# Token differences ahead of their rounding, seven-product blocks on PSUM copies, and attention squares added on GpSimd

## Chip, core and metric

One core of one Trainium2 chip runs the whole program: TensorE (PE in the profile, with its weight loads as PEld), VectorE (DVE), ScalarE (ACT), GpSimd (POOL), and SyncE (SP), whose queue issues the transfers from HBM. The metric is the device time of one execution in microseconds (us). Every number is fp32; a fp32 product is made here as three products of a faster type (below).

## The reference, cut to what matters

One layer: 128 context tokens and 512 latent tokens of 1024 features. The changed places are the sum of squares of the attention's output (the first `_rms` of the mixer) and the SwiGLU network.

```
def _rms(x, g):
    return x * rsqrt(mean(x * x, axis=-1) + 1e-6) * g

# mixer: attn (tokens x 512) and y_conv (tokens x 512) are normed apart, joined and projected
merged = concat([_rms(attn, attn_out_norm), _rms(y_conv, conv_out_norm)])
x = x + g1 * (merged @ w_out)

# feed-forward: w_gate_up 1024 x 5632, w_down 2816 x 1024
h2 = _rms(x, norm_ffn) * (1 + sc2) + sh2
gate, up = split(h2 @ w_gate_up, 2)
x = x + g2 * ((silu(gate) * up) @ w_down)
```

## The kernel before

**Products.** Each fp32 operand is held as a high part, rounded by ACT (L151: `hi = Copy(src)` into type fp32r), and a low part, made by DVE (L152: `lo = src - hi`). `mm3` (L154 to L157) issues hi·hi, hi·lo and lo·hi into one PSUM tile. So every operand costs one ACT and one DVE instruction before TensorE may use it.

**Stages.** The preamble makes the conditioning and the input projections. Then comes the attention stage, with the convolution's products as filler between the attention's steps. After it come the output projection with its residual and the second norm (L1083 to L1147), and the feed-forward part (from L1159) until the end. Tokens go in five blocks of 128: four latent ones, t = 0 to 3, and the context, t = 4.

**What sets the order.** TensorE's order is the order of the program text; in the attention stage it is a list of steps written out by hand (`SEQ`: scores `S`, transposes `T`, value products `O`, filler `F`, sums of squares `r`). On the other engines a scheduler orders instructions by priority; `with early(n)` raises that priority. DVE's order is by hand only from the first feed-forward block until the second call of `b_sums`. Weights go through one list, `order`: `W(key)` gives an entry's tiles and, on the way, loads entries up to `AOP` places further on. An entry is a transfer (rings `w`, `f`) or, for the ring `op`, an operand that `op_load` makes out of weights that lie in SBUF already. Raw weights have three buffers (`wf`); high and low parts have four each (`wh`, `wl`).

**Sums of squares.** For each token block and each half v of the heads, `att_add` (L885) adds two halves of the attention's output on DVE (L895), one after a swap of partitions by DMA, and squares the result on ACT into two of the four 128 x 128 quarters of `osq` (L896; for token block 3 the tile is named `oz`). At step `r`, `att_rms` (L942) sums the squares over the features: four products of 128 x 1 with a vector of ones (L945, two PE rows each, since they stay fp32). DVE scales the sum, and POOL raises it to the power -1/2 (L165). There are five such sites: steps r4, r0, r1, r2 in `SEQ`, and token block 3 in the output projection. POOL otherwise adds the convolution's squares (L758).

**Feed-forward blocks.** The 2816 hidden columns go in 22 blocks f of 128, in four groups (0 to 5, 6 to 11, 12 to 16, 17 to 21). After a group, `down` (L1240) multiplies its hidden values `gT` by `w_down`. A block's weights are two transfers of 512 KB, the gate columns g and the up columns u. Each is cut along the contracted features into A11, A12 (of g) and A21, A22 (of u), four chunks of 128 x 128 each. Tokens are cut into two halves of 320, LO and HI, which gives quarters B11, B21 (LO) and B12, B22 (HI) of the normed input. Blocks 0 and 1 are **plain** (`plain`, L1167): four products A11·B11 + A12·B21 and A21·B11 + A22·B21 for LO, later the same four for HI. From block 2 on, seven products do for eight, in Strassen's manner in Winograd's form: A11·B11, S1·T1, S2·T2, A12·B21, S3·T3, A22·T4, S4·B22. S1 to S4 are sums of A's (`op_load`: L206 on DVE, then the rounding by L151 and L152 on 512-wide tiles). T1 to T4 are differences of B's (`b_sums`, L1071: DVE's difference L1078, ACT's rounding L1064, DVE's low part L1065), made once, in two parts of the token range, tokens 128 to 319 and 0 to 127 of each half. `prod` (L1162) issues one product as four `mm3` with 320 columns, 12 PE rows.

A seven-product block runs on TensorE as `ff_a` (A11·B11 into PSUM tile b1), `ff_c` (S1·T1 into b3), `ff_d` (S2·T2 added to b1), `ff_b` (A12·B21 into b2) and `ff_e` (S3·T3 added to b1, A22·T4 into b4, S4·B22 added to b3). Between them ACT copies what b1 holds at three moments into SBUF (`copy_of`, L1193 to L1196: p1, u2, u3; the profile calls these tiles p and u). DVE adds these to the other products: L1209 `cg = b2 + p1`, L1225 `cu = b3 + u3`, L1228 `cu = b4 + u3`, and L1235 `cg = b3 + u2` in `ff_end`, which is called in the next block behind `ff_c`. ACT applies Silu to cg, DVE multiplies it with cu, and `ff_out` (L1184) rounds the result into gT. PSUM has six tiles for all this (`FB`).

## Time and profile before

| | |
|---|---|
| median of 3 runs | 755.47 us (754.89 to 755.61) |
| the profiled execution | 755.84 us |
| its span | 754.0 us |
| mean granted clock of TensorE | 0.999 |
| PE busy | 735.5 us, 98% |
| PEld busy | 661.6 us, 88% |
| DVE busy | 553.2 us, 73% |
| ACT busy | 378.7 us, 50% |
| POOL busy | 42.7 us, 6% |
| 16 DMA engines, hardware queue q1 | 36.5% |

The profile is one execution on the chip. Each instruction is a row: start in us from the span's beginning, duration, engine, line (L), operation, output `<-` inputs by the program's names, shape, and in brackets the engine's idle time before it with what ended it. `x4` says that a row of the time line stands for four instructions. Matmuls are pipelined and their ends are modelled, so starts are surer than ends. The span leaves out 1.8 us of the execution around it (755.84 - 754.0).

### The profile page before, as it was taken

Reading aid. Unit: us, or ns where it says so; the run is one execution under the profiler, and the core shown is the slowest. Engines: PE = TensorE matmul, PEld = TensorE weight load, DVE = VectorE, ACT = ScalarE, POOL = GpSimd, SP = SyncE. Lnnn points to the kernel's source line nnn. Section 1 sums busy time; section 2 is a strip of 40 time slices with the busy share of each in tenths; the row PEclk is TensorE's granted clock in tenths of the full one; section 3 lists DMA queues with packets and bytes.
Section 4 is the critical chain, followed back from the end, with each engine's and each line's share of the span. In section 5 each row is a group of like instructions: output and inputs, shape, how many; then the busy total and the mean of one; then the engine's idle time right before and its main releaser. Section 6 shows DMA issues by size and latency. Waiting matters only on the chain.

```text
span 754.0 us, 11900 instructions
## 1 busy us (share of the span) xinstructions
PE 735.5 (98%) x4586; PEld 661.6 (88%) x4586; DVE 553.2 (73%) x1009; ACT 378.7 (50%) x745; POOL 42.7 (6%) x75
## 2 busy tenths in 40 slices
PE   7999899999999999999999999999999999999997
PEld 6668788988988887899998799998889998899986
DVE  5668877666666798779979778884678866788653
ACT  5356777667666534765552135553125541255410
POOL 2403101011000110100000000000000000000000
PEclk9999999999999999999999999999999999999999
DMA  9985133532432464031335223223113132122312
GB/s 290 297 242 155 47 107 97 170 92 91 143 123 91 133 240 123 1 112 56 87 110 178 87 63 106 76 94 112 56 56 109 60 112 82 58 87 83 112 56 84
DMA packets 101389, 84.52 MB, mean 112 GB/s; under 512 B 3502, under 2 KB 81650, under 8 KB 101332
## 3 DMA queue, kind: packets, MB, share of 16 engines
q1 hardware_dynamic: 100980, 83.39, 36.5%
q8 instruction: 36, 0.59, 0.3%
q0 software_dynamic: 352, 0.37, 0.2%
q14 instruction: 21, 0.17, 0.1%
HBM read 79.68 MB, written 2.75 MB: 109 GB/s over the span
## 4 chain that ended last, share of the span: by engine, by line
PE 82%; DVE 8%; ACT 5%; DMA 3%; issue 1%; SPq 0%; POOL 0%; ACTq 0%; DVEq 0%
PE pf L155 17%; PE pf L156 17%; PE pf L157 17%; PE pc L717 3%; PE pc L719 3%; PE pc L718 3%; PE ph L155 2%; PE ph L156 2%; PE ph L157 2%; PE po L873 2%; PE ps L829 2%; PE pt L856 2%; PE pc L388 2%; DMA es<-t 1%; ACT pr L839 1%
## 5 line engine op out<-in xcount | busy, mean ns | idle before, releaser
L151 ACT ACTIVATE wh<-wf 128x512 fp32r<-128x512 f32 (+1 forms) x68 | 55.5, 816 | 81.5 <-PE pf L157 59.9
L155 PE MATMUL pf<-wh,gT 128*128 128x512 f32 (+1 forms) x225 | 86.9, 386 | 0.0
L156 PE MATMUL pf<-wl,gT 128*128 128x512 f32 (+1 forms) x225 | 86.5, 385 | 0.0
L157 PE MATMUL pf<-wh,gT 128*128 128x512 f32 (+1 forms) x225 | 86.5, 384 | 0.0
L717 PE MATMUL pc<-hH,wh 128*128 128x320 f32 x192 | 61.1, 318 | 0.0
L719 PE MATMUL pc<-hH,wl 128*128 128x320 f32 x192 | 59.3, 309 | 0.0
L718 PE MATMUL pc<-hL,wh 128*128 128x320 f32 x192 | 59.3, 309 | 0.0
L152 DVE TENSOR_TENSOR wl<-wf,wh 128x1024 fp32r<-128x1024 f32 (+1 forms) x34 | 39.4, 1160 | 24.9 <-ACT wh L151 21.8
L155 PE MATMUL pf<-T,wh 128*128 128x320 f32 x160 | 49.6, 310 | 0.6 <-ACT u L1196 0.5
L155 PEld LDWEIGHTS pf<-wh,gT 128*128 128x128 f32 x225 | 42.3, 188 | 8.6 <-ACT wh L151 0.2
L157 PEld LDWEIGHTS pf<-wh,gT 128*128 128x128 f32 x225 | 42.3, 188 | 8.5
L156 PEld LDWEIGHTS pf<-wl,gT 128*128 128x128 f32 x225 | 42.3, 188 | 8.4 <-issue 0.2
L155 PE MATMUL pf<-T,wl 128*128 128x320 f32 x160 | 49.4, 309 | 0.0
L156 PE MATMUL pf<-T,wl 128*128 128x320 f32 x160 | 49.4, 309 | 0.0
L157 PE MATMUL pf<-T,wl 128*128 128x320 f32 x160 | 49.4, 309 | 0.0
L156 PE MATMUL pf<-T,wh 128*128 128x320 f32 x160 | 49.4, 309 | 0.0
L157 PE MATMUL pf<-T,wh 128*128 128x320 f32 x160 | 49.4, 309 | 0.0
L155 PE MATMUL pf<-B,wl 128*128 128x320 f32 x152 | 47.1, 310 | 0.0
L157 PE MATMUL pf<-B,wl 128*128 128x320 f32 x152 | 47.0, 309 | 0.0
L156 PE MATMUL pf<-B,wl 128*128 128x320 f32 x152 | 47.0, 309 | 0.0
L155 PE MATMUL pf<-B,wh 128*128 128x320 f32 x136 | 42.2, 310 | 1.5 <-DVE cu L1225 1.5
L1275 DVE TENSOR_TENSOR dm<-pf,g 128x512 f32<-128x512 f32 (+1 forms) x41 | 27.7, 676 | 21.1 <-PE pf L157 21.1
(306 smaller groups left out, 2049.6 us busy)
## 6 DMA issues: line engine op xcount, KB each, us to landing
wf<-in_w_gate_up_dram SPq DMA_DIRECT2D x44, 512.0 KB, 3.9
aw<-in_w_ada_dram SPq DMA_DIRECT2D x24, 512.0 KB, 4.0
wf<-in_w_down_dram SPq DMA_DIRECT2D x20, 512.0 KB, 3.3
wf<-in_w_in_dram SPq DMA_DIRECT2D x18, 512.0 KB, 5.9
af<-in_w_ada_dram SPq DMA_DIRECT2D x32, 256.0 KB, 6.5
x<-in_x_sample_dram SPq DMA_DIRECT2D x8, 512.0 KB, 5.8
wf<-in_w_out_dram SPq DMA_DIRECT2D x8, 512.0 KB, 4.4
wf<-in_w_ada_dram SPq DMA_DIRECT2D x8, 512.0 KB, 3.8
```

The lines of the kernel that those rows point to most:

```text
L151: act.activation(hi, src, AF.Copy)
L152: dve.tensor_tensor(lo, src, f32(hi), ALU.subtract)
L155: pe.matmul(out, lh, rh, start=start, stop=False, skip_group_check=more)
L156: pe.matmul(out, lh, rl, start=False, stop=False, skip_group_check=more)
L157: pe.matmul(out, ll, rh, start=False, stop=stop, skip_group_check=more)
L388: pe.matmul(out[CG * g:CG * (g + 1)], cp[:, k], w, start=(k < 4), stop=(k >= KD - 4), skip_group_check=True)
L717: pe.matmul(acc, wh[:, k], hH[k][:, c0:c0 + n], start=(k == 0), stop=False)
L718: pe.matmul(acc, wh[:, k], hL[k][:, c0:c0 + n], start=False, stop=False)
L719: pe.matmul(acc, wl[:, k], hH[k][:, c0:c0 + n], start=False, stop=(k == KD - 1))
L829: pe.matmul(s2[:, g, :320], q, kk[:, v, P + g * 320:P + (g + 1) * 320], start=(i == 0), stop=(i == 1))
L856: pe.transpose(tp[:, i, h], u[3][h][:, kt * P:(kt + 1) * P], ident)
L1275: dve.tensor_tensor(dm, ps[:, :n], g2[cc][:, oc], ALU.mult)
```

## The change

Three things change.

1. **`b_sums`**: the difference of the next T is made before the rounding of the one before: T1, T2, round T1, T3, round T2, T4, round T3, round T4. The arithmetic stays.
2. **Operands and seven-product blocks.** Operands are made two at a time, in 1024-wide tiles: `A1` (all of g), `A2` (all of u), `S12`, `S34`; only A22 of a seven-product block stays 512 wide. `PAIRS` finds the half. A block of seven products now has four entries of `op` instead of seven, a plain one two instead of four, and `AOP` falls from 9 to 6. In the block, ACT copies b1 behind A11·B11 **into PSUM**, to b2, and A12·B21 adds to it there; Silu reads b2 itself. ACT likewise copies b1 behind S3·T3 into b4, and A22·T4 adds to it; DVE's product reads b4 itself. S1·T1 is copied into SBUF (p5) before S4·B22 adds to b3, and the HI half of cu is b1 + p5. The adds L1209 and L1228 are gone. S4·B22 now runs ahead of A22·T4.
3. **`att_add`, `att_rms`**: after the second half's squares, POOL adds the four quarters to one (256 wide, then 128 wide), and `att_rms` issues one product instead of four.

```diff
 FEND = 2
-AOP = 9
+AOP = 6
 NPLAIN = 2
...
         if name[0] == "S":
-            if name == "S1":
-                sums[f] = T("sx", (P, 2, 4, P), F32, 2)
-            s13, s24 = sums[f][:, 0], sums[f][:, 1]
-            src, x, y, op = {"S1": (s13, a21, a22, ALU.add), "S2": (s24, s13, a11, ALU.subtract),
-                             "S3": (s13, a11, a21, ALU.subtract), "S4": (s24, a12, s24, ALU.subtract)}[name]
+            if name == "S12":
+                sums[f] = T("sx", (P, 8, P), F32, 2)
+            s13, s24 = sums[f][:, 0:4], sums[f][:, 4:8]
             with early(SOP[f >= NPLAIN]):
-                (pool if f < SPO else dve).tensor_tensor(src, x, y, op)
+                for out, x, y, op in {"S12": ((s13, a21, a22, ALU.add), (s24, s13, a11, ALU.subtract)),
+                                      "S34": ((s13, a11, a21, ALU.subtract), (s24, a12, s24, ALU.subtract))}[name]:
+                    dve.tensor_tensor(out, x, y, op)
+            src = sums[f]
         else:
-            src = {"A11": a11, "A12": a12, "A21": a21, "A22": a22}[name]
-        w = T(("wh", "wl")[ops[0] % 2], (P, 2, 4, P), F32R, WHB)
-        ops[0] += 1
+            src = {"A1": g, "A2": u, "A22": a22}[name]
+        if name == "A22":
+            w = T(("wh", "wl")[ops[0] % 2], (P, 2, 4, P), F32R, WHB)
+            ops[0] += 1
+            e[5] = w[:, 0], w[:, 1]
+        else:
+            e[5] = T("wh", (P, 8, P), F32R, WHB), T("wl", (P, 8, P), F32R, WHB)
         with early(SOP[f >= NPLAIN]):
-            split(w[:, 0], w[:, 1], src)
-        e[5] = w
+            split(*e[5], src)
...
     GROUPS = [list(range(a, b)) for a, b in zip(GCUT, GCUT[1:])]
-    PLAIN, PRODS = ("A11", "A12", "A21", "A22"), ("A11", "S1", "S2", "A12", "S3", "A22", "S4")
+    PLAIN, PRODS = ("A1", "A2"), ("A1", "S12", "S34", "A22")
+    PAIRS = {"A11": ("A1", 0), "A12": ("A1", 4), "A21": ("A2", 0), "A22": ("A2", 4),
+             "S1": ("S12", 0), "S2": ("S12", 4), "S3": ("S34", 0), "S4": ("S34", 4)}
...
         act.activation(osq[t][:, 2 * v:2 * v + 2], o, AF.Square)
+        if v:
+            q = osq[t]
+            pool.tensor_tensor(q[:, 0:2], q[:, 0:2], q[:, 2:4], ALU.add)
+            pool.tensor_tensor(q[:, 0], q[:, 0], q[:, 1], ALU.add)
         if t == CTX:
...
         sps = PB((P, 1))
-        for p in range(4):
-            pe.matmul(sps, osq[t][:, p], ones[:, 0:1], start=(p == 0), stop=(p == 3))
+        pe.matmul(sps, osq[t][:, 0], ones[:, 0:1], start=True, stop=True)
         rA[t] = rstd_of(sps, 1, 1.0 / 512, tag="rA")
...
         b11, b12, b21, b22 = (quarter(x, part) for x in ("B11", "B12", "B21", "B22"))
-        last = None
-        for x in ("T1", "T2", "T3", "T4"):
-            w = T("tr", (P, 4, 192), F32, 3)[:, :, :n]
-            y, z = {"T1": (b12, b11), "T2": (b22, last), "T3": (b22, b12), "T4": (b21, last)}[x]
-            dve.tensor_tensor(w, y, z, ALU.subtract)
-            b_put(x, w, part)
-            if x != "T3":
-                last = w
+        w = {}
+
+        def diff(x, y, z):
+            w[x] = T("tr", (P, 4, 192), F32, 3)[:, :, :n]
+            dve.tensor_tensor(w[x], y, z, ALU.subtract)
+
+        diff("T1", b12, b11)
+        diff("T2", b22, w["T1"])
+        b_put("T1", w["T1"], part)
+        diff("T3", b22, b12)
+        b_put("T2", w["T2"], part)
+        diff("T4", b21, w["T2"])
+        b_put("T3", w["T3"], part)
+        b_put("T4", w["T4"], part)
...
     open_pool("Y2", "left", "B22 T1 T2 T3 T4")
-    open_pool("G", "right", "cg cu p1 u2 u3 dm tr")
+    open_pool("G", "right", "cg cu p5 u2 dm tr")
     gT, st, pair = {}, {}, [None]
...
     def prod(out, f, a, b, start=True, stop=True, more=False):
-        w = W(("op", f, a))
+        x, k0 = PAIRS[a] if f < NPLAIN or a != "A22" else (a, 0)
+        wh, wl = W(("op", f, x))
         for k in range(4):
-            mm3(out[:, :HALF], w[:, 0, k], w[:, 1, k], *B[b][k], start and k == 0, stop and k == 3, more)
+            mm3(out[:, :HALF], wh[:, k0 + k], wl[:, k0 + k], *B[b][k], start and k == 0, stop and k == 3, more)
...
     def ff_a(f):
-        b1 = FB()
+        b1, b2 = FB(), FB()
         prod(b1, f, "A11", "B11")
-        cg = T("cg", (P, TOK), F32, 2)
-        st[f] = [b1, copy_of("p1", b1), cg, None, None, None, None]
+        with early(CPP):
+            act.activation(b2[:, :HALF], b1[:, :HALF], AF.Copy)
+        st[f] = [b1, b2, T("cg", (P, TOK), F32, 2), None, None, None]
     def ff_b(f):
-        b2 = FB()
-        prod(b2, f, "A12", "B21")
-        b1, p1, cg = st[f][0:3]
-        dve.tensor_tensor(cg[:, LO], b2[:, :HALF], p1, ALU.add)
-        act.activation(cg[:, LO], cg[:, LO], AF.Silu)
+        b2, cg = st[f][1:3]
+        prod(b2, f, "A12", "B21", start=False, more=True)
+        act.activation(cg[:, LO], b2[:, :HALF], AF.Silu)
     def ff_c(f):
-        st[f][3] = FB()
-        prod(st[f][3], f, "S1", "T1")
+        b3 = st[f][3] = FB()
+        prod(b3, f, "S1", "T1")
+        st[f][4] = copy_of("p5", b3)
...
         prod(st[f][0], f, "S2", "T2", start=False, more=True)
-        st[f][4] = copy_of("u2", st[f][0])
+        st[f][5] = copy_of("u2", st[f][0])
     def ff_e(f):
-        b1, _, cg, b3, u2 = st[f][0:5]
+        b1, _, cg, b3, p5, u2 = st[f]
         prod(b1, f, "S3", "T3", start=False, more=True)
-        u3 = copy_of("u3", b1)
+        b4 = FB()
+        with early(CPP):
+            act.activation(b4[:, :HALF], b1[:, :HALF], AF.Copy)
         cu = T("cu", (P, TOK), F32, 2)
-        dve.tensor_tensor(cu[:, HI], b3[:, :HALF], u3, ALU.add)
-        b4 = FB()
-        prod(b4, f, "A22", "T4")
-        dve.tensor_tensor(cu[:, LO], b4[:, :HALF], u3, ALU.add)
-        dve.tensor_tensor(cu[:, LO], cu[:, LO], cg[:, LO], ALU.mult)
+        dve.tensor_tensor(cu[:, HI], b1[:, :HALF], p5, ALU.add)
         prod(b3, f, "S4", "B22", start=False, more=True)
+        prod(b4, f, "A22", "T4", start=False, more=True)
+        dve.tensor_tensor(cu[:, LO], b4[:, :HALF], cg[:, LO], ALU.mult)
         st[f] = cg, cu, b3, u2
...
     def ff_end(f):
```

The first place where the order of instructions moves is DVE's first preparation of T, around block 0's products (`tr` is a difference, `T1` to `T4` the low parts of the rounded differences, gT_712 and gT_713 hold quarters of the normed input). Before:

```order
L1078 TENSOR_TENSOR tr_849_3984<-gT_712_3273 128x768
L1065 TENSOR_TENSOR T1_850_3986<-tr_849_3984,T1_850_3986 128x4x192
L1078 TENSOR_TENSOR tr_851_3989<-gT_713_3274,tr_849_3984 128x768
L1065 TENSOR_TENSOR T2_852_3991<-tr_851_3989,T2_852_3991 128x4x192
L1078 TENSOR_TENSOR tr_853_3994<-gT_713_3274,gT_712_3273 128x768
L1065 TENSOR_TENSOR T3_854_3996<-tr_853_3994,T3_854_3996 128x4x192
L1078 TENSOR_TENSOR tr_855_3999<-gT_713_3274,tr_851_3989 128x768
L1065 TENSOR_TENSOR T4_856_4001<-tr_855_3999,T4_856_4001 128x4x192
```

The same place now (line numbers in rows of the changed kernel are those of its own file; L1087 is the difference, L1074 the low part):

```order
L1087 TENSOR_TENSOR tr_849_3971<-gT_712_3271 128x768
L1087 TENSOR_TENSOR tr_850_3973<-gT_713_3272,tr_849_3971 128x768
L1074 TENSOR_TENSOR T1_851_3975<-tr_849_3971,T1_851_3975 128x4x192
L1087 TENSOR_TENSOR tr_852_3978<-gT_713_3272,gT_712_3271 128x768
L1074 TENSOR_TENSOR T2_853_3980<-tr_850_3973,T2_853_3980 128x4x192
L1087 TENSOR_TENSOR tr_854_3983<-gT_713_3272,tr_850_3973 128x768
L1074 TENSOR_TENSOR T3_855_3985<-tr_852_3978,T3_855_3985 128x4x192
L1074 TENSOR_TENSOR T4_856_3988<-tr_854_3983,T4_856_3988 128x4x192
```

Each low part now has the next difference between itself and its own difference.

The second place is ACT in block 3. Before, from the copy behind A11·B11 (p1_904) to the copy behind S2·T2 (u2_910); cg_884 is block 2's Silu, gT_908 the rounding of its hidden values, and the wl and wh rows round operands of blocks 3 and 4:

```order
L1196 ACTIVATE p1_904_4366<-pf_899_4345 128x320
L1236 ACTIVATE cg_884_4234<-cg_884_4234 128x320
L151 ACTIVATE wl_907_4371<-sx_906_4369 128x512
L151 ACTIVATE gT_908_4389<-cu_895_4309 128x640
L151 ACTIVATE wh_909_4393<-sx_906_4369 128x512
L1196 ACTIVATE u2_910_4408<-pf_899_4345 128x320
L151 ACTIVATE wl_912_4411<-wf_900_4346 128x512
```

And now, from the copy of b1 into b2 (pf_899) to the copy of b1 into b4 (pf_914); wl_897 is A22 of block 3, wh_907 the rounding of S1 and S2 of block 4, cg_904 block 3's Silu:

```order
L1219 ACTIVATE pf_899_4319<-pf_898_4318 128x320
L151 ACTIVATE wl_897_4302<-wf_883_4199 128x512
L1252 ACTIVATE cg_886_4218<-cg_886_4218 128x320
L1212 ACTIVATE p5_909_4362<-pf_905_4342 128x320
L151 ACTIVATE gT_910_4367<-cu_896_4288 128x640
L151 ACTIVATE wh_907_4346<-sx_906_4343 128x1024
L1212 ACTIVATE u2_911_4382<-pf_898_4318 128x320
L1225 ACTIVATE cg_904_4341<-pf_899_4319 128x320
L1241 ACTIVATE pf_914_4415<-pf_898_4318 128x320
```

Ahead of u2 there now stands one rounding of 1024 columns, of both S1 and S2 of the next block, where there were roundings of 512.

The third place is POOL from the sum of token block 0 to that of token block 2 (rA is the power -1/2 of an attention sum, rB that of the convolution's). Before:

```order
L165 TENSOR_TENSOR rA_633_2867<-ms_632_2865,neghalf_40_176 128x1
L758 TENSOR_TENSOR ysum_174_735<-ysum_174_735,c25_709_3234 128x512
L758 TENSOR_TENSOR ysum_174_735<-ysum_174_735,c25_709_3234 128x128
L165 TENSOR_TENSOR rB_726_3329<-ms_725_3327,neghalf_40_176 128x5
L165 TENSOR_TENSOR rA_748_3411<-ms_747_3409,neghalf_40_176 128x1
```

And now:

```order
L905 TENSOR_TENSOR osq_563_2524<-osq_563_2524 128x256
L906 TENSOR_TENSOR osq_563_2524<-osq_563_2524 128x128
L165 TENSOR_TENSOR rA_633_2863<-ms_632_2861,neghalf_40_176 128x1
L764 TENSOR_TENSOR ysum_174_735<-ysum_174_735,c25_709_3230 128x512
L764 TENSOR_TENSOR ysum_174_735<-ysum_174_735,c25_709_3230 128x128
L905 TENSOR_TENSOR oz_665_3019<-oz_665_3019 128x256
L906 TENSOR_TENSOR oz_665_3019<-oz_665_3019 128x128
L165 TENSOR_TENSOR rB_726_3327<-ms_725_3325,neghalf_40_176 128x5
L165 TENSOR_TENSOR rA_748_3406<-ms_747_3404,neghalf_40_176 128x1
```

Two adds stand ahead of each attention power, and those of token block 3 (oz) behind the convolution's adds.

## The prediction

> **What bounds the kernel now.** The page comes first: where the span goes, and which engine the chain that ended last runs through.
>
> ```profile
> span 754.0 us, 11900 instructions
> PE 735.5 (98%) x4586; PEld 661.6 (88%) x4586; DVE 553.2 (73%) x1009; ACT 378.7 (50%) x745; POOL 42.7 (6%) x75
> PE 82%; DVE 8%; ACT 5%; DMA 3%; issue 1%; SPq 0%; POOL 0%; ACTq 0%; DVEq 0%
> ```
>
> TensorE is the bound. A change can win here only by taking rows out of its queue, or by taking a wait out of it. The table by stretches shows which of the changed stages have waits (columns: PE, PEld, DVE, ACT, POOL busy, clock, DMA share, GB/s).
>
> ```profile
> 120.00:200.00 80.00, 79.83 (x572) 71.61 (x570) 51.95 (x105) 55.05 (x120) 7.02 (x14) 1.00 0.35 111
> 345.00:365.00 20.00, 17.97 (x119) 17.18 (x118) 19.78 (x36) 12.13 (x24) 0.00 (x0) 1.00 0.20 58
> 365.00:420.00 55.00, 55.00 (x331) 51.70 (x330) 46.71 (x75) 22.65 (x39) 0.00 (x0) 1.00 0.49 147
> ```
>
> The attention (120 to 200) and the later seven-product blocks (from 365) keep TensorE full. Only the first seven-product block, block 2, lies in a stretch where TensorE stands still for 2 us, and there DVE is full: 19.78 of 20. TensorE's own waits name the places:
>
> ```profile
> PE pf L155 <- DVE cu L1225: 1.5, 1, 1.5
> PE pf L155 <- ACT u L1196: 0.5, 1, 0.5
> PE pt L945 <- ACT osq L896: 0.4, 1, 0.4
> ```
>
> A matmul's end in the record is modelled, so the true price of the first two is read from the starts of block 2's products (first row of each, in the order A11, S1, S2, A12, S3, A22, S4, then the next block):
>
> ```profile
> 348.77 0.31 PE L155 MATMUL pf<-B,wh 128*128 128x320 f32 x1
> 350.53 0.31 PE L155 MATMUL pf<-T,wl 128*128 128x320 f32 x1
> 352.49 0.42 PE L155 MATMUL pf<-T,wh 128*128 128x320 f32 x1
> 354.36 0.31 PE L155 MATMUL pf<-B,wl 128*128 128x320 f32 x1
> 356.80 0.42 PE L155 MATMUL pf<-T,wh 128*128 128x320 f32 x1 [0.52 <-ACT u L1196]
> 358.65 0.31 PE L155 MATMUL pf<-T,wl 128*128 128x320 f32 x1
> 362.05 0.42 PE L155 MATMUL pf<-B,wh 128*128 128x320 f32 x1 [1.47 <-DVE cu L1225]
> 363.91 0.31 PE L155 MATMUL pf<-B,wl 128*128 128x320 f32 x1
> ```
>
> An undisturbed product takes 350.53 - 348.77 = 1.76 us. The others exceed it by 0.20 (S2 late), 0.11, 0.68 (S3 late), 0.09, 1.64 (S4 late) and 0.10 (the slower rows after each wait): **2.82 us** in all. That is everything the seven-product part can give back.
>
> **Part 1: one sum-of-squares product instead of four.** The last of the five sites (token block 3), and the site of token block 2, where TensorE waited:
>
> ```profile
> 269.36 0.95 PE L945 MATMUL pt<-ones,oz 128*128 128x1 f32 x8
> 270.17 0.48 PE L155 MATMUL ph<-wh,mx 128*128 128x512 f32 x1
> 224.90 0.50 PE L945 MATMUL pt<-ones,osq 128*128 128x1 f32 x4
> 225.77 0.61 PE L945 MATMUL pt<-ones,osq 128*128 128x1 f32 x4 [0.37 <-ACT osq L896]
> 226.24 0.36 PE L873 MATMUL po<-ph,VS 128*128 128x256 f32 x1
> 225.30 0.41 ACT L896 ACTIVATE osq<-of 128x256 f32<-128x256 f32 x1
> 265.34 0.42 ACT L896 ACTIVATE oz<-of 128x256 f32<-128x256 f32 x1 [3.61 <-DVE of L895]
> ```
>
> Each site issues 8 rows (two for each fp32 product) in 270.17 - 269.36 = 0.81 us, 0.10 us a row. Six rows go at each: 0.61 us. At four sites the squares are ready long before TensorE asks, so I count 4 x 0.61 = **-2.43 us**. What follows those sites there (scores, row maximum, exponential) starts from TensorE's own rows, so it moves along with it.
>
> The new GpSimd adds are not in the trace; its adds on the convolution's squares are the nearest rows (512 and 128 wide, by form, and the pair on the time line).
>
> ```profile
> L758 POOL TENSOR_TENSOR ysum<-ysum,c 128x512 f32<-128x512 f32 x3 | 4.7, 1583 | 67.4 <-ACT c L756 67.4
> L758 POOL TENSOR_TENSOR ysum<-ysum,c 128x128 f32<-128x128 f32 x3 | 1.6, 528 | 0.0
> 216.04 1.73 POOL L758 TENSOR_TENSOR ysum<-ysum,c 128x512 f32<-128x512 f32 x2 [19.30 <-ACT c L756]
> 174.06 2.24 POOL L758 TENSOR_TENSOR ysum<-ysum,c 128x512 f32<-128x512 f32 x2 [17.00 <-ACT c L756]
> 173.50 1.23 DVE L152 TENSOR_TENSOR wl<-wf,wh 128x1024 fp32r<-128x1024 f32 x1 [0.39 <-ACT wh L151]
> ```
>
> A straight line through 528 and 1583 ns gives 0.88 us at 256 wide; with the 128-wide add, 1.41 us. The bounds are 384/640 of the pair's 1.73 us, 1.04, and its slow case, 2.24. I take 1.41, which lies between like rows. At the site of token block 2 nothing covers it: the squares end at 225.71, the adds at about 227.20 (0.08 us to start), and with 0.06 us to wake TensorE and two rows of 0.10 the next product starts at 227.46 instead of 226.24: **+1.22 us** (0.85 to 2.05 by the bounds). Behind TensorE's new wait stand the last value product of a unit and the next scores; DVE's scale of the sum waits there too, as it does now. At the other sites the cover is larger; the least is at token block 3, whose squares end at 265.76 and whose product starts at 269.36, 3.6 us, more than the adds at their slowest.
>
> The row at 174.06 took 0.51 us longer than the one at 216.04, and beside it DVE ran a subtraction with two SBUF operands. The Trainium skill (SBUF — State Buffer, section "SBUF: two separate sides") says that such a DVE instruction and a GpSimd instruction that reads SBUF lock each other out for a whole instruction; by it this site could cost as much more as the longest such subtraction, 1.23 us, and the sum would be -2.0 instead of -3.2. That rule fits the two rows, but DVE has only a reciprocal and a scale in that moment, so I keep the sum.
>
> **Part 2: differences ahead of their rounding.** DVE around block 2's preparation, and the late instructions:
>
> ```profile
> 331.78 0.95 DVE L1078 TENSOR_TENSOR tr<-gT 128x768 f32<-128x768 f32 x1
> 333.64 0.96 DVE L1065 TENSOR_TENSOR T<-tr,T 128x768 fp32r<-128x768 f32 x1 [0.91 <-ACT T L1064]
> 334.52 0.95 DVE L1078 TENSOR_TENSOR tr<-gT,tr 128x768 f32<-128x768 f32 x1
> 342.73 0.68 DVE L152 TENSOR_TENSOR wh<-wf,wh 128x512 fp32r<-128x512 f32 x1
> 353.95 0.69 DVE L206 TENSOR_TENSOR sx<-wf,sx 128x512 f32<-128x512 f32 x1
> 361.51 0.49 DVE L1225 TENSOR_TENSOR cu<-pf,u 128x320 f32<-128x320 f32 x1
> 338.21 0.31 PE L155 MATMUL pf<-gT,wh 128*128 128x320 f32 x1
> ```
>
> Now each T costs 334.52 - 331.78 = 2.74 us, of which 0.91 is waiting for ACT's rounding; four take until 342.73. In the new order another difference fills each wait: eight instructions at 0.88 us (333.64 to 334.52), 7.0 us, done at 338.8, 3.9 us earlier. The next work, block 2's A1, can't be much earlier than that: its buffer is one that block 0's second-half products read until 338.21. DVE's queue from 342.73 to S4, the last sum of block 2 (353.95), is 11.2 us of work with next to no wait; about 1 us of it can go ahead, so S4 starts near 350 to 351 instead.
>
> **Part 3: the seven-product blocks.** The forms:
>
> ```profile
> L152 DVE TENSOR_TENSOR wl<-wf,wh 128x1024 fp32r<-128x1024 f32 x20 | 24.5, 1223 | 22.0 <-ACT wh L151 20.7 <-PE pf L157 1.3
> L151 ACT ACTIVATE wh<-wf 128x1024 fp32r<-128x1024 f32 x20 | 21.2, 1060 | 49.6 <-PE pf L157 35.9 <-DMA wf<-in_w_down_dram 9.1 <-issue 2.6
> L1196 ACT ACTIVATE u<-pf 128x320 f32<-128x320 f32 x40 | 17.4, 436 | 30.8 <-PE pf L157 30.8
> wf<-in_w_gate_up_dram SPq DMA_DIRECT2D x8, 512.0 KB, 3.9
> ```
>
> TensorE's products are as many and as long as before. DVE loses two adds of 0.49 us in each block and three instruction starts; ACT gets a fourth copy and three rounding starts fewer. Both have room (46.71 and 22.65 of 55), so this is worth nothing by itself. The waits of block 2 change thus. S4 no longer waits for a DVE add (361.51) but for ACT's copy p5, four products old: 1.74 us go. S3 waits for u2, which now stands behind ACT's rounding of A1(3), released by the same product: 0.95 + 0.44 = 1.4 us, less than the 1.76 us of A12 that covers it. S2's copy stands behind T4's rounding, and that now comes earlier with DVE. So 2.82 us go.
>
> A copy that ACT writes into PSUM has no row; the bounds are L1196's 0.44 us and twice that, and I take 0.44, a copy of equal size out of the same memory. S4 (1.76 us) covers the copy that A22 waits for, so at twice the price it shows only where ACT starts it late, 0.4 us a place. No reading below nothing: a faster copy frees nothing that waits.
>
> **What is late next** is block 3's u2. In the new order it stands behind the rounding of S1 and S2 of block 4, which needs those sums, which need up(4) landed; that transfer waits for a buffer that S4's sum of block 3 gives back. With every product at 1.76 us, S3(3) is due at 368.13. The step before: u(3) is asked for after S4(2), 351.6, lands at 355.5 (3.9 us); then A1(3), the sums and S12(3) on DVE and ACT put S4(3)'s end at 361.7; up(4) lands at 365.65; S1, a product and S2 on DVE take until 367.3; the rounding lets go at 368.35, and u2 ends at 368.8. S3(3) waits 0.7 us, 0.8 with the slower rows behind it: **+0.8 us**. From block 4 on DVE has caught up: a block takes TensorE 7 x 1.76 = 12.3 us, and in the stretch from 365 on DVE is busy 46.71 of 55, before it loses two adds of 0.49 a block. I count nothing there.
>
> **Sum.** -2.43 + 1.22 - 2.82 + 0.8 = **-3.2 us** on the profiled execution's 755.84 us (span 754.0 and 1.8 around it): 752.6. That execution lies 0.37 above the median of the runs shown, 755.47; with it the median becomes 752.3, and I say **752.4**.
>
> **Rivals.**
> - All gains, no new wait: up(4) lands earlier or the adds are at their short bound: -2.43 + 0.85 - 2.82 = -4.4, with a shorter wake-up -4.8: 750.7. For it: DVE has 8 us to spare in each later stretch.
> - The attention swallows its part: after a freed slot TensorE only waits longer for an exponential. Then part 1 is +1.22 alone, the whole -0.8: 754.7, no change. For it: two of the chain's engines there are DVE and ACT; against it: 79.83 of 80.
> - **Slower**: u2 stands behind a 1024-wide rounding in each of the 16 blocks that have a successor in their group, and the wait of block 3 comes back in all: 15 more times 0.8 is +12, sum +8.8: 764.3. It decides from 0.31 us a block on (4.7 us over 15). Against it: DVE's slack from 365 on.
>
> **How the numbers follow.** Chances: forecast 0.52, all gains 0.13, swallowed 0.17, slower 0.18. A measurement of this kernel tells about 0.2%, 1.5 us, from no change. Faster is the first two, 0.65; same 0.17; slower 0.18. The range, 750.0 to 755.6, holds the first three cases with the bounds of the adds (-0.4, +0.8) and leaves out the slower one and a little on both sides.
>
> **What would show it.** Two L945 rows at each site, about 0.2 us; a wait for POOL near 223 of 1.4 us or more; block 2's products at 1.76 us each; T4's first rounding some 4 us earlier relative to T1's; one wait of S3 for ACT's u2 in block 3. The forecast is wrong if S3 waits in many blocks, if TensorE waits more for exponentials, or if the adds take over 2 us.

## The result, and the profile after

The changed kernel takes **755.34 us** (median of 12, 753.98 to 756.18) against 755.17 (median of 12, 754.83 to 755.61): ratio 0.9999, 95% interval 0.9990 to 1.0008. **No difference**, where 752.4 was forecast. Its times lie further apart than before, 2.2 us against 0.8. Its profiled execution took 756.18 us. Of its page, the span, the busy times and the chain's shares:

```profile
span 754.4 us, 11635 instructions
PE 732.7 (97%) x4556; PEld 657.7 (87%) x4556; DVE 530.2 (70%) x905; ACT 374.9 (50%) x701; POOL 49.5 (7%) x85
PE 78%; DVE 7%; DMA 6%; ACT 5%; issue 2%; SPq 1%; POOL 1%; ACTq 0%; DVEq 0%
```

TensorE was relieved by 2.8 us (735.5 to 732.7) and DVE by 23, but the span is no shorter: TensorE waits for what it no longer works. The same three stretches as before:

```profile
120.00:200.00 80.00, 79.75 (x569) 71.25 (x571) 53.22 (x108) 56.33 (x122) 9.40 (x18) 1.00 0.36 114
345.00:365.00 20.00, 18.41 (x126) 18.15 (x125) 16.14 (x26) 10.25 (x17) 0.00 (x0) 1.00 0.19 53
365.00:420.00 55.00, 54.36 (x326) 50.93 (x326) 44.12 (x63) 23.32 (x38) 0.00 (x0) 1.00 0.45 141
```

DVE at block 2 fell from 19.78 to 16.14 of 20, and yet TensorE stands still there for 1.6 us. Its waits, largest new ones:

```profile
PE pt L954 <- POOL osq L906: 1.9, 1, 1.9
PE pf L155 <- ACT pf L1241: 1.6, 1, 1.6
PE ph L156 <- DVE wl L252: 0.7, 2, 0.4
PE pf L155 <- ACT u L1212: 0.6, 1, 0.6
```

The DVE add is gone from this list (it was 1.5), and four waits have come: for GpSimd's adds at token block 2, for ACT's copy ahead of A22 in block 2, for weight parts in the output projection, and for u2 in block 3. Only the first and the last had been forecast.

**Block 2.** First rows of its products in the order A11, S1, S3, S4, A22, and of block 3's A11:

```profile
349.49 0.31 PE L155 MATMUL pf<-B,wh 128*128 128x320 f32 x1
351.25 0.31 PE L155 MATMUL pf<-T,wh 128*128 128x320 f32 x1
356.53 0.31 PE L155 MATMUL pf<-T,wh 128*128 128x320 f32 x1
358.29 0.31 PE L155 MATMUL pf<-B,wh 128*128 128x320 f32 x1
361.80 0.41 PE L155 MATMUL pf<-T,wh 128*128 128x320 f32 x1 [1.59 <-ACT pf L1241]
363.66 0.31 PE L155 MATMUL pf<-B,wh 128*128 128x320 f32 x1
```

From A11 to S4 five products take 8.80 us, 1.76 each: every old wait is gone. Then A22 comes 1.75 us late. What held it, on SP, DVE and ACT:

```profile
352.26 0.37 SPq L228 DMA_DIRECT2D wf<-in_w_gate_up_dram  x1
357.90 0.69 DVE L206 TENSOR_TENSOR sx<-wf 128x512 f32<-128x512 f32 x1 [2.02 <-DMA wf<-in_w_gate_up_dram]
360.37 1.06 ACT L151 ACTIVATE wh<-sx 128x1024 fp32r<-128x1024 f32 x1 [3.20 <-DVE sx L206]
361.33 0.42 ACT L1241 ACTIVATE pf<-pf 128x320 f32<-128x320 f32 x1
```

The transfer of block 3's up columns, issued at 352.26, was first used at 357.90, 5.64 us later. DVE's sum, then ACT's 1024-wide rounding of it wait for it, and the copy that A22 needs (the last row of S3 starts before 358.29) stands in ACT's queue behind that rounding until 361.33.

**Token block 2.** GpSimd's adds and TensorE's sum:

```profile
224.33 0.72 POOL L905 TENSOR_TENSOR osq<-osq 128x256 f32<-128x256 f32 x1 [7.78 <-ACT osq L902]
225.14 0.45 POOL L906 TENSOR_TENSOR osq<-osq 128x128 f32<-128x128 f32 x1
225.64 0.38 PE L954 MATMUL pt<-ones,osq 128*128 128x1 f32 x2 [1.86 <-POOL osq L906]
```

The pair takes 1.26 us (224.33 to 225.59), where 1.41 was estimated.

**Token block 3 and behind it.** DVE's second add of the attention's halves, its two accumulations for the gate, the convolution's sum of squares, and the first mix that needs GpSimd's power of it; before, then now:

```profile
264.89 0.42 DVE L895 TENSOR_TENSOR of<-t,es 64x256 f32<-64x256 f32 x1
265.34 1.42 DVE L1034 SCALAR_TENSOR_TENSOR aacc<-wf,cs,aacc 128x512 f32<-128x512 f32 x2
266.77 0.16 DVE L163 TENSOR_SCALAR ms<-pt 128x5 f32<-128x5 f32 x1
268.74 0.75 DVE L1123 SCALAR_TENSOR_TENSOR mix<-ph,rB,mix 128x512 f32<-128x512 f32 x1 [1.08 <-POOL rB L165]
```

```profile
265.07 0.42 DVE L901 TENSOR_TENSOR of<-t,es 64x256 f32<-64x256 f32 x1
265.52 1.90 DVE L1043 SCALAR_TENSOR_TENSOR aacc<-wf,cs,aacc 128x512 f32<-128x512 f32 x2
267.45 0.15 DVE L163 TENSOR_SCALAR ms<-pt 128x5 f32<-128x5 f32 x1
269.45 0.75 DVE L1138 SCALAR_TENSOR_TENSOR mix<-ph,rB,mix 128x512 f32<-128x512 f32 x1 [1.08 <-POOL rB L165]
```

GpSimd in the same moment, and TensorE's wait at the end of that chain, in the second half of the output projection:

```profile
266.02 0.85 POOL L905 TENSOR_TENSOR oz<-oz 128x256 f32<-128x256 f32 x1 [5.83 <-ACT oz L902]
266.95 0.80 POOL L906 TENSOR_TENSOR oz<-oz 128x128 f32<-128x128 f32 x1
```

```profile
292.31 0.50 PE L156 MATMUL ph<-wl,mx 128*128 128x512 f32 x1 [0.35 <-DVE wl L252]
```

DVE is 0.18 us later than before at its second add and 0.71 later at the first mix. In between, the same two accumulations took 1.90 instead of 1.42 us beside GpSimd's adds. DVE has little room from there on (busy 18.44 of 20 us from 260 to 280, 18.02 from 280 to 300), and the last weight part that TensorE waits for is made 0.61 us late (291.51 for 290.90). TensorE had come 1.00 us early (288.63 for 289.64, four rows into these products) and leaves the place 0.61 late (292.31 for 291.70), as late as DVE. Before the change the row at 291.70 started 0.06 us behind the end of that weight part (290.90 + 0.74 = 291.64), so TensorE had nothing to spare here: what it gains ahead of this place is kept only if DVE's chain comes as much earlier.

### The profile page after: what moved, and what is told of

Read it like the earlier page. It is cut to its first block, busy times and chain, and to the rows that moved or that the text cites. A ratio compares the mean times of both kernels' runs of the same rounds, so it can differ in the third digit from the quotient of the medians.

```text
span 754.4 us, 11635 instructions
## 1 busy us (share of the span) xinstructions
PE 732.7 (97%) x4556; PEld 657.7 (87%) x4556; DVE 530.2 (70%) x905; ACT 374.9 (50%) x701; POOL 49.5 (7%) x85
## 4 chain that ended last, share of the span: by engine, by line
PE 78%; DVE 7%; DMA 6%; ACT 5%; issue 2%; SPq 1%; POOL 1%; ACTq 0%; DVEq 0%
PE pf L155 17%; PE pf L156 17%; PE pf L157 17%; PE pc L723 3%; PE pc L724 3%; PE pc L725 3%; PE ps L835 2%; PE po L879 2%; PE pt L862 2%; DMA es<-t 2%; PE pc L394 2%; DMA af<-in_w_ada_dram 2%; DMA wf<-in_w_gate_up_dram 1%; PE ph L156 1%; PE ph L157 1%
## 5 line engine op out<-in xcount | busy, mean ns | idle before, releaser
L151 ACT ACTIVATE wh<-wf 128x1024 fp32r<-128x1024 f32 (+1 forms) x68 | 65.6, 968 | 86.2 <-PE pf L157 45.6
L155 PE MATMUL pf<-B,wh 128*128 128x320 f32 x288 | 89.3, 310 | 0.0
L157 PE MATMUL pf<-B,wl 128*128 128x320 f32 x288 | 89.3, 310 | 0.0
L156 PE MATMUL pf<-B,wh 128*128 128x320 f32 x288 | 89.2, 310 | 0.0
L157 PE MATMUL pf<-T,wl 128*128 128x320 f32 x280 | 86.7, 310 | 0.0
L151 ACT ACTIVATE wh<-sx 128x1024 fp32r<-128x1024 f32 x40 | 42.4, 1060 | 82.9 <-PE pf L157 49.8
L152 DVE TENSOR_TENSOR wl<-sx,wh 128x1024 fp32r<-128x1024 f32 x40 | 48.9, 1224 | 27.4 <-ACT wh L151 23.8
L155 PEld LDWEIGHTS pf<-T,wh 128*128 128x128 f32 x280 | 52.6, 188 | 2.7 <-ACT pf L1241 1.8
L157 PEld LDWEIGHTS pf<-B,wl 128*128 128x128 f32 x288 | 54.1, 188 | 0.1
L155 PEld LDWEIGHTS pf<-B,wh 128*128 128x128 f32 x288 | 54.1, 188 | 0.1
L156 PEld LDWEIGHTS pf<-B,wh 128*128 128x128 f32 x288 | 54.1, 188 | 0.1
L156 PEld LDWEIGHTS pf<-T,wh 128*128 128x128 f32 x280 | 52.6, 188 | 0.0
L157 PEld LDWEIGHTS pf<-T,wl 128*128 128x128 f32 x280 | 52.6, 188 | 0.0
```

The lines of the kernel that those rows point to most:

```text
L151: act.activation(hi, src, AF.Copy)
L152: dve.tensor_tensor(lo, src, f32(hi), ALU.subtract)
L155: pe.matmul(out, lh, rh, start=start, stop=False, skip_group_check=more)
L156: pe.matmul(out, lh, rl, start=False, stop=False, skip_group_check=more)
L157: pe.matmul(out, ll, rh, start=False, stop=stop, skip_group_check=more)
```

## The experiments

Each kernel is compared with the kernel before on its own chip, whose median was 755.44 to 755.53. Two stretches of the profiles place the differences: from the first sum of squares (116.53 in the profile before) to the first of the products on aacc, what the two accumulations for the gate go into (292.26), and from block 2's A11 (348.77) to the last product. Each cell is how much longer the stretch is than before, from the start times of the same TensorE rows in both traces. The last two columns are block 3's up transfer, from its issue to DVE's first use, and A22's wait in block 2. What a kernel's two stretches don't show lies mostly in the preamble, whose pieces differ by up to 1.25 us from one execution to another. With the forms only, DVE had no idle time ahead of that first use, so its 6.92 us are DVE's lateness and not the transfer's.

| kernel | ratio to before (95%) | sums of squares to aacc | block 2 to end | up transfer | A22 waits |
|---|---|---|---|---|---|
| changed | 0.9999 (0.9990 to 1.0008) | -0.10 | -0.35 | 5.64 | 1.59 |
| changed, again | 1.0002 (0.9993 to 1.0011) | +0.73 | -1.96 | 3.77 | 0 |
| adds only | 1.0015 (1.0006 to 1.0024) | +1.55 | -0.27 | | |
| no adds | 0.9979 (0.9970 to 0.9989) | -0.29 | -2.09 | 3.69 | 0 |
| blocks 2 and 3 without adds | 0.9971 (0.9959 to 0.9982) | -1.37 | -0.93 | 4.76 | 0.71 |
| block 2 without adds | 0.9978 (0.9969 to 0.9987) | -1.31 | -1.17 | 4.62 | 0.56 |
| block 3 without adds | 0.9997 (0.9988 to 1.0006) | +0.97 | -1.37 | 4.36 | 0.31 |
| A22 on its own in block 2 | 0.9995 (0.9986 to 1.0004) | +1.17 | -0.17 | 5.60 | 0 |
| differences only | 0.9982 (0.9973 to 0.9991) | -0.01 | -1.15 | | |
| forms only | 0.9993 (0.9984 to 1.0002) | -0.04 | -1.25 | 6.92 | 0 |
| sum of block 2 later | 0.9974 (0.9963 to 0.9986) | -1.70 | -1.33 | 4.38 | 0.33 |
| the same, block 3 without adds | 0.9963 (0.9950 to 0.9975) | -2.34 | -0.93 | 4.68 | 0.62 |
| products in the wait | 0.9997 (0.9989 to 1.0006) | +0.29 | -0.91 | 4.78 | 0.73 |

### The change in two halves

Adds only: the third part put into the kernel before.

```diff
+        if v:
+            q = osq[t]
+            pool.tensor_tensor(q[:, 0:2], q[:, 0:2], q[:, 2:4], ALU.add)
+            pool.tensor_tensor(q[:, 0], q[:, 0], q[:, 1], ALU.add)
...
-        for p in range(4):
-            pe.matmul(sps, osq[t][:, p], ones[:, 0:1], start=(p == 0), stop=(p == 3))
+        pe.matmul(sps, osq[t][:, 0], ones[:, 0:1], start=True, stop=True)
```

> The kernel before with the third part of the change alone (GpSimd adds the squares, one sum-of-squares product at each of five sites). My forecast's sum for this part was -1.2 us, so about 754.0. Theory A (the gain is swallowed behind the attention, in the output projection, by DVE's chain, which the swap transfer of token block 3, its squares, GpSimd's adds and GpSimd's power for the convolution start): TensorE runs about 1.7 us ahead of before at the end of the attention and gives it back by the second half of the output projection, in waits for DVE's and ACT's weight parts there: within 0.3 us of before, 754.9 to 755.5. Rival B (the adds disturb the attention itself): slower than before by 0.5 us or more, with longer waits inside the attention.

756.71 us against 755.53: 1.1 us slower (0.5 to 1.8). The forecast's -1.2 is refuted, and so is theory A in its plain form: the gain isn't only swallowed, there is a loss.

No adds: the same diff taken out of the changed kernel.

> The changed kernel without the third part: four sum-of-squares products at each site as before, the order of the token differences and the new blocks kept. The forecast's sum for these parts was -2.0 us, about 753.2. Theory A (block 2's three old waits go, but A22 of block 2 waits some 1.7 us for ACT's copy into PSUM, which stands behind a 1024-wide rounding that waits for up columns of block 3, and S3 of block 3 some 0.7): -0.4 us or so, 754.5 to 755.0. Rival C (the 1024-wide roundings and PSUM copies cost a little in every block): 755.5 or more, with waits spread over blocks 4 to 21.

753.63: 1.6 us faster (0.8 to 2.3). The forecast's -2.0 for these two parts holds, and theory A's -0.4 does not. A22 doesn't wait here; of block 2's old waits none is left; and S3 of block 3 waits for u2, as forecast:

```profile
368.68 0.42 PE L155 MATMUL pf<-T,wh 128*128 128x320 f32 x1 [0.75 <-ACT u L1209]
```

So the loss sits in the adds.

### Which site

Two sites kept: GpSimd adds at the context and at token blocks 0 and 1 alone.

```diff
-        if v:
+        if v and t not in (2, 3):
...
-        pe.matmul(sps, osq[t][:, 0], ones[:, 0:1], start=True, stop=True)
+        n = 4 if t in (2, 3) else 1
+        for p in range(n):
+            pe.matmul(sps, osq[t][:, p], ones[:, 0:1], start=(p == 0), stop=(p == n - 1))
```

> The changed kernel with GpSimd's adds at the context and at token blocks 0 and 1 only; token blocks 2 and 3 keep their four products. Theory A: the wait of 1.9 us at token block 2 becomes 0.4, GpSimd's power for the convolution starts at once, and DVE's two accumulations beside it take 1.4 us again instead of 1.9; TensorE's wait for weight parts in the second half of the output projection ends 0.5 to 0.7 us earlier: 0.5 to 0.7 below the changed kernel, about 754.7. Rival (GpSimd's queue and adds there have no part in that wait, it is the transfer of weights): the wait stays where it is in time, no difference to the changed kernel within 0.2 us, since what the two sites lose or win is swallowed there.

753.60, 2.2 us below before (1.4 to 3.1), some three times as far below the changed kernel as theory A had it. The three sites' gain, forecast at 1.83 us and measured at 1.98 (from the first sum to the row ahead of token block 2's: 106.24 us for 108.22), now passes the output projection for the greater part (-1.37). The next two part the sites.

Block 2 kept (`t != 2` and `n = 4 if t == 2 else 1` in the diff above):

> The changed kernel with token block 2 alone back at four products; the other four sites keep GpSimd's adds. It parts the loss of the two sites. Theory K (the loss is the clock: TensorE stands still some 2 us at token block 2, longer than the 0.4 of before, and in two of three profiles was then granted half its clock for about 3 us): no wait over 0.5 us there, no drop of the clock, 753.5 to 754.0. Theory Q (GpSimd's queue: the adds of token block 3 stand ahead of the convolution's power, whose result DVE's chain through the output projection waits for): 0.5 us or more of the gain stays lost there, with a wait for weight parts near 290, and the time is 754.0 to 754.7, above that of the kernel with both sites kept (753.6).

Block 3 kept (the same with 3):

> The changed kernel with token block 3 alone back at four products; the adds of token block 2 stay. Theory K: the wait of about 2 us at token block 2 stays, with the clock at half behind it in some executions: 754.5 to 755.5, and times further apart than those of the kernel with both sites kept. Theory Q: most of the loss was GpSimd's queue at token block 3, so 753.7 to 754.3.

753.80 and 754.90. Theory K had both figures, theory Q neither: with four products at token block 2 alone the kernel is 1.6 us faster than the changed one. But the adds at the other four sites then bring nothing over no adds at all (ratios 0.9978 and 0.9979), where the forecast had -2.43 for them. The traces show where that stays. From the row behind token block 3's sum to the products on aacc TensorE takes 22.00 to 22.15 us in the four profiles without adds (before, no adds, differences only, forms only), 22.25 to 22.81 in the three with adds at other sites alone, and 23.38 to 24.10 in all seven with adds at token block 3. So the output projection takes back 1.3 to 2.0 us with adds there, and some of the gain even without them. What stands behind the wait at token block 2 is seen in the second profile of the changed kernel.

### The changed kernel again

> The changed kernel once more, on this chip, as the measure for the three others, and for a second profile. 755.0 to 755.6. Theory K: if its profile shows a wait of 1.9 us or more at token block 2 followed by a granted clock near 0.5 for some 3 us, the drop belongs to this kernel too and its first profile was one of the executions without it. The transfer of block 3's up columns taken from its issue to DVE's first use, less 4.05 us, gives the wait of A22 in block 2 (0.3 to 1.6 us in five profiles).

755.41 us, 754.03 to 757.91. Here TensorE's wait, and the granted clock (third number from the right) in the stretches of 1 us behind it:

```profile
225.18 0.38 PE L954 MATMUL pt<-ones,osq 128*128 128x1 f32 x2 [2.04 <-POOL osq L906]
```

```profile
225.00:226.00 1.00, 0.82 (x6) 0.82 (x7) 0.16 (x1) 0.05 (x1) 0.29 (x2) 0.95 0.00 0
226.00:227.00 1.00, 1.00 (x6) 0.96 (x5) 0.08 (x1) 0.33 (x1) 0.39 (x1) 0.50 0.06 16
228.00:229.00 1.00, 1.00 (x6) 1.00 (x5) 0.59 (x1) 0.93 (x3) 0.00 (x0) 0.50 0.00 0
229.00:230.00 1.00, 1.00 (x8) 1.00 (x6) 0.79 (x2) 1.00 (x3) 0.00 (x0) 0.84 0.00 0
```

For 3.41 us the clock is at half. The first profile of the changed kernel, after a wait of 1.86 us, has 1.00 in each of these stretches; its stretch to aacc is 0.83 us shorter. The profiles with adds only (a wait of 1.98), with A22 on its own (2.33) and with block 3 without adds (2.04) all show the drop, 0.83 over the stretch from 225 to 235 us, and are the other three above +0.7 in the table. Where no adds stand at token block 2, or its sum is asked for later, no profile shows it there. Its price in the profiles is clear: from the row behind token block 2's sum to token block 3's sum TensorE takes 44.11 to 44.50 us in the four with the drop, and 43.13 to 43.19 in the eight others whose sum stands in the old place.

The times do not show that price. The mean granted clock of every execution is on record, and one such drop takes 0.0023 off it; the drop behind the last products, seen in several profiles, takes 0.0013 at most. So 0.999 or 1.000 means no drop at token block 2, and 0.998 or less means one somewhere. In the five measurements with the whole wait (changed, changed again, adds only, A22 on its own, block 3 without adds) 43 of 56 executions have 0.998 or less. In the first of the changed kernel they are 7 of 12, with a median of 755.46 us against 755.21 for the 5 without a drop, and 11 of 11 in this second measurement. Compared within each of the five, executions without a drop are no faster on average (0.0 us, with 0.6 to either side). The mean does not say where a drop lies: three profiles (adds only, two sites kept, and the last kernel of "The place of the sum") show one at 19.0 to 19.7 us, in the preamble. So the half clock and its 1.0 us are shown in four profiles, but not that it makes the executions slower.

The Trainium skill (TensorE: Matmul & The Clock Gate, section "Part 1: The HAM clock gate (the "warmup" mystery)") has the array's clock at half after an idle window of about 3.4 us, the windows running free of the program. The half and the length of the slow stretch, 3.41 us, agree; here 1.98 us of standing still sufficed, so the idle time need not be a whole window's.

### Work in the wait

Six products of the identity with itself ahead of that sum, into the tile that it overwrites.

```diff
+NDUM = 6
...
-        sps = PB((P, 1))
+        if t == 2:
+            wide = PB((P, P))
+            for _ in range(NDUM):
+                pe.matmul(wide, ident, ident, start=True, stop=True)
+            sps = wide[:, 0:1]
+        else:
+            sps = PB((P, 1))
```

> The changed kernel with six products of the identity with itself put on TensorE ahead of the sum of squares of token block 2, into a PSUM tile whose first column that sum then overwrites; nothing that is computed changes. They fill the wait with some 1.5 us of work. Theory K (half of the loss at that place is the clock, granted at half after about 2 us of standing still): the wait is cut to 0.5 us, the clock stays at 1.0 there in every execution, and the time falls though TensorE has more to do: 0.6 to 1.2 us below the changed kernel on this chip, with times closer together. Rival (the clock has no part, only the wait): the same as the changed kernel within 0.3 us, or slower by what the products take beyond the wait.

```profile
224.20 1.50 PE L957 MATMUL pt<-ident 128*128 128x128 f32 x12
226.18 0.38 PE L961 MATMUL pt<-ones,osq 128*128 128x1 f32 x2 [0.48 <-POOL osq L907]
```

The wait is 0.48 us and the clock stays at 1.00. The time is 755.20, 0.2 us below the changed kernel on that chip and with less spread (754.46 to 756.53). The profile agrees with theory K, and so does the clock on record: 3 of 11 executions have a mean of 0.998 or less, where the changed kernel had 11 of 11. But the time does what the rival had, the same within 0.3 us, and not the 0.6 to 1.2 us of theory K. The ratios' intervals overlap, so a smaller gain isn't excluded. With the drop the stretch to aacc is 0.73 to 1.55 us longer than before, without it -0.10 and +0.29.

### The place of the sum

```diff
-       ... O12.1 F1 F1 r2 O12.2 S14.0 T13.0 T13.1 F1 S14.1 F1 F1 T13.2 F1 ...
+       ... O12.1 F1 F1 O12.2 S14.0 T13.0 T13.1 F1 S14.1 F1 F1 r2 T13.2 F1 ...
```

> The changed kernel with one step moved in the order written out by hand: the sum of squares of token block 2 (r2) is asked for some 4 us of TensorE's work later, behind the next scores and filler, so that GpSimd's adds are covered. Theory K (the loss at token block 2 is the place: a wait of about 2 us, and the clock at half behind it): no wait for GpSimd and no drop of the clock, and the 0.4 us that the kernel before waited there goes too: 753.0 to 753.8, 1.5 us or more below the changed kernel on this chip. Rival (the adds themselves are the loss, wherever they stand): less than 0.7 us below it.

753.22, 2.0 us below before (1.1 to 2.8) and 2.2 below the changed kernel's median on that chip. TensorE waits for GpSimd nowhere. With token block 3 at four products as well:

> As the one before, and token block 3 back at four products, so that GpSimd's power for the convolution no longer stands behind adds. The candidate for the best version. Theory Q: another 0 to 0.5 us, 752.5 to 753.5, 2.0 to 3.0 below the kernel before; waits for weight parts near 290 are shorter than in the one before by 0.4 us or more. Rival (that queue costs nothing): 0.2 us above the one before or more, since three products more are issued at token block 3.

**752.55, 2.8 us below before (1.9 to 3.8), the lowest median of all.** Its interval overlaps with that of the one before it, so the two aren't told apart by time; in the profile the waits for weight parts near 290, 0.8 us in the one before, are gone. DVE at token block 3:

```profile
262.89 0.42 DVE L901 TENSOR_TENSOR of<-t,es 64x256 f32<-64x256 f32 x1
263.34 1.42 DVE L1045 SCALAR_TENSOR_TENSOR aacc<-wf,cs,aacc 128x512 f32<-128x512 f32 x2
266.74 0.75 DVE L1140 SCALAR_TENSOR_TENSOR mix<-ph,rB,mix 128x512 f32<-128x512 f32 x1 [1.08 <-POOL rB L165]
```

From the second add to the first mix 3.85 us, as before the change (268.74 - 264.89); with the adds it is 4.38 in the changed kernel (269.45 - 265.07). All seven profiles with adds at token block 3 have 4.38, and all seven without have 3.85. So theory Q had the site but not the mechanism: rB starts about 0.25 us behind the start of its input with and without adds (267.01 behind 266.77, 267.71 behind 267.45), so GpSimd's queue holds it by some hundredths at most. Its input is late, since DVE's accumulations take 1.90 instead of 1.42 beside GpSimd's adds. The three pairs of kernels with and without these adds (0.9978 and 0.9971, 0.9999 and 0.9997, 0.9974 and 0.9963) all go that way in time, but no pair is told apart by itself.

### A22 without the copy

In block 2 alone A22·T4 starts its own tile, and DVE adds u3 from SBUF.

```diff
+        own = f == 2
+        if own:
+            u3 = copy_of("u3", b1)
...
-        prod(b4, f, "A22", "T4", start=False, more=True)
+        prod(b4, f, "A22", "T4", start=own, more=not own)
+        if own:
+            dve.tensor_tensor(cu[:, LO], b4[:, :HALF], u3, ALU.add)
+            dve.tensor_tensor(cu[:, LO], cu[:, LO], cg[:, LO], ALU.mult)
...
```

> The changed kernel, but in block 2 alone A22 times T4 starts its own PSUM tile, u3 goes to SBUF and DVE adds it, as before the change. Theory A (A22 of block 2 waits for ACT's copy behind the rounding of block 3's sums): that wait goes, 1.0 to 1.7 us below the changed kernel, about 754.0. Rival (the 1.7 us were one slow transfer of that one execution, 5.6 us instead of 3.8): 0.3 us or less below it; then the profile of this run shows block 3's up columns landing in under 4 us.

755.11: not told from the changed kernel. But the rival isn't right either: the transfer was as slow as in the first profile (issued 353.04, used 358.64), A22 didn't wait, and the delay came out in block 3, at A12's copy and at u2:

```profile
353.04 0.37 SPq L228 DMA_DIRECT2D wf<-in_w_gate_up_dram  x1
358.64 0.69 DVE L206 TENSOR_TENSOR sx<-wf 128x512 f32<-128x512 f32 x1 [1.97 <-DMA wf<-in_w_gate_up_dram]
367.52 0.41 PE L155 MATMUL pf<-T,wh 128*128 128x320 f32 x1 [1.25 <-ACT pf L1219]
372.47 0.42 PE L155 MATMUL pf<-T,wh 128*128 128x320 f32 x1 [1.17 <-ACT u L1212]
```

The two together, 2.42, stand against 1.59 and 0.64 in the changed kernel. A wait was moved, not taken away. In the seven profiles in which A22 waits, its wait is the transfer's time less 4.05 us to a few hundredths; at 3.69 and 3.77 there is none. So it is the transfer that sets it. (In the kernel with the forms only ACT comes to the copy ahead of that rounding, so A22 is not held there.)

### The other two parts alone

Differences only: the new `b_sums` in the kernel before.

> The kernel before with the second part alone: the new order of the token differences, old blocks, old sums of squares. Theory D (block 2's waits come from DVE being late, which this part alone mends): DVE reaches block 2's sums some 3 us earlier, all three waits go, and block 3 has no new one, since no 1024-wide rounding stands ahead of its u2: 752.5 to 753.3. Rival (S4's wait for the DVE add stays, since that add stands behind other operand work in DVE's queue): 1 us gained or less, 754.4 to 755.2.

754.01, 1.4 us faster (0.7 to 2.0). Between the two: S4's wait goes, but S2 of block 2 now waits for the copy p1, behind a rounding of T on ACT:

```profile
353.10 0.41 PE L155 MATMUL pf<-T,wh 128*128 128x320 f32 x1 [0.85 <-ACT p L1202]
```

Forms only: the new blocks with the old `b_sums`, no adds.

> The changed kernel's blocks alone: operands two at a time, partials copied into PSUM, but the old order of the token differences and four sum-of-squares products. Theory D: DVE is as late as before at block 2, S2 and S3 wait as before or longer, S4 no longer waits for a DVE add, and block 3's sums and u2 are late by up to 3 us more: no gain, 754.5 to 756. Rival (the copies are what frees block 2): 753.5 to 754.2, as the kernel with the new differences and the new blocks has it.

754.89, 0.5 us faster, with zero inside the interval (-1.2 to +0.2): within theory D's range, though its profile shows S4 free and 1.3 us of waits for u2 in blocks 2 and 3.

## Where the prediction held and where it failed, point by point

755.34 lies inside the stated range, 750.0 to 755.6, but near its slow end and not by the merit of the sum: 752.4 was forecast, and faster had a chance of 0.65. "No change" stood there for the rival in which the attention swallows its part. Something of that kind happened, at another place and by another mechanism, so it is luck that the number lies in the range.

- **What bounds the kernel**: right. TensorE's rows went by 2.8 us, and only waits decide what that is worth.
- **Four sites, -2.43**: right on TensorE's own rows, wrong on what is left of them. Three sites gave some 1.97 us in every profile with adds there, and the fourth 0.67. The scores and exponentials swallowed nothing: from the row behind token block 2's sum to token block 3's the time is 43.13 us before and 43.14 in the first profile after. The step that failed is "at the other sites the cover is larger". It covered TensorE's product only. Behind token block 3 the output projection runs at the pace of DVE's chain, with 0.06 us to spare before the change, and the adds there slow that chain by 0.5 us. TensorE gave back 1.61 and 1.29 us there in the two profiles of the changed kernel.
- **The site of token block 2, +1.22**: the wait was sized well, +0.93 to +1.40 between the neighbouring rows in five profiles. The half clock behind it, 1.0 to 1.4 us in four of them, was not in the sum, and the executions' times don't confirm it. By time the site is worth 1.6 us, not told from 1.22, so this isn't the term that decides: with it out, the forecast's sum is -4.4 us, and the kernel with block 2 kept was 1.7 us faster than before (1.0 to 2.3).
- **The rule of the Trainium skill** (SBUF — State Buffer, section "SBUF: two separate sides"), weighed at token block 2 and set aside for what DVE did there: it bears on token block 3. The accumulations read two SBUF operands, and the second of them takes 1.23 us in all seven profiles with adds there and 0.75 in all seven without. By the rule's whole-instruction lock it could have been more; 0.48 is measured.
- **Block 2's three waits, -2.82**: right. They went in every kernel with both parts, and the kernel without adds has -2.09 from there to the end, where -2.0 was forecast.
- **The copy that A22 waits for**, "0.4 us a place" at most: wrong by its queue, not by its length (0.42 measured, 0.44 taken). It stands behind a rounding that waits for the up transfer, as u2 does in block 3, where I had seen the same thing. I gave that transfer its median, 3.9 us, and there it takes 3.69 to 5.64; from 4.05 us on TensorE pays the difference.
- **Block 3's u2, +0.8**: right, 0.64 to 1.00 in the kernels with both parts and the copies, apart from the one in which a wait was moved there.

In the forecast's own terms, by the two profiles of the changed kernel: the four sites -2.64, token block 2's wait +0.93 and +1.10, the half clock 0 and +0.98, the output projection +1.61 and +1.29. That is -0.10 and +0.73 up to aacc, where -1.2 was forecast. From block 2 on it is -0.35 and -1.96, where -2.0 was forecast; A22 waited 1.59 us in the first and not in the second. How the miss of 3.1 us in the medians divides among these terms isn't settled by the times.

## What to carry to other kernels

A gain on TensorE is worth what the next place at which another engine sets the pace lets through; look for that place, and for how little TensorE has to spare there, before counting saved rows in full. A few instructions saved aren't worth a wait of 2 us, and moving the waiting step behind other work gave 2 us here for nothing. An engine off the path can still be paid for: look at what runs beside its new work, and at what stands in its queue, not only at when its result is needed. And where a copy stands in a queue behind work that waits for a transfer, count that transfer at its slowest, since freeing one consumer only moves the wait to the next.

## What the runs showed of the hardware

- After 1.98, 2.04, 2.04 and 2.33 us without work TensorE's granted clock was 0.50 for 3.41 us; after 1.86 us it was not. Three profiles show a drop of the same length in the preamble, where the longest single wait of TensorE just before was 1.06 to 1.22 us. Whether the length or the moment decides, these can't tell.
- GpSimd's add took 0.72 us for 128x256 and 0.45 for 128x128 at token block 2, 0.85 and 0.80 at token block 3 beside DVE's accumulations, of which the second took 1.23 us instead of 0.75.
- ACT's copy from PSUM to PSUM took 0.42 us for 128x320, as much as u2's from PSUM to SBUF (0.42); p5's took 0.44.
- The same 512 KB transfer took 3.69 to 5.64 us from issue to first use in ten profiles of kernels with the new differences and blocks, with no pattern that I found; its cause was not tried.
